# A hybrid decoder block on one core: first steps of the mixer, logits and routing in another order, quad 0's gate tiles cut in 4 KB runs, six tiles queued at the branch

## The chip, the cores and the metric

The kernel runs on one core of a Trainium2 chip. The time is the device time of one execution in microseconds (us). TensorE (PE) multiplies, VectorE (DVE) and ScalarE (ACT) work elementwise, GpSimd (POOL) and SyncE (SP) do side work; both of the last also issue DMA transfers here. Each engine takes its own instructions in the order in which they were laid down, and waits for others through semaphores.

## The reference

For 256 tokens x 1024 the block computes, all in float32 (g_mix, g_sgu, g_ffn, g_ple and g_final are the norms' gains):

```
h = rmsnorm(x, g_mix);  z = h @ w_in
b, c, xin, u, v = split(z, 5 parts of 512)
y_conv = b * conv3(c * xin, w_conv)
y_sgu  = gelu(u) * (causal w_spatial @ layernorm(gelu(v), g_sgu) + b_spatial)
x = x + concat(y_conv, y_sgu) @ w_out
t = rmsnorm(x, g_ffn);  g_prob = softmax(t @ w_group + b_group);  top 1 of 4 groups
e_logits = t @ w_router + b_router;  top 2 of the 8 experts in that group; softmax
x = x + sum over 32 experts of comb * ((silu(t @ w_gate) * (t @ w_up)) @ w_down)
x = x + sigmoid(rmsnorm(x, g_ple) @ w_ple_gate) * (p @ w_ple_proj)
out = rmsnorm(x, g_final)
```

Each expert has a gate and an up matrix of 1024 x 512 and a down matrix of 512 x 1024: 6 MB, and 192 MB for the 32 of them. All are read, whatever the routing.

## The kernel before, in words

**Mixer.** The tokens lie in two tiles (t = 0, 1) of 128 rows. Lines 200 to 211 norm them: ScalarE squares and sums a row block (L204), VectorE and GpSimd make the reciprocal root `rstd` (L114, L115), VectorE scales the identity by it (`diag`, L207), and 16 matmuls with `diag` transpose and scale the tokens at once into `pht` (L210). From `pht` come `hh` and `hl`, a high and a low part (L215, L216); weights are split likewise into `wh` and `wl` by ScalarE and VectorE (or GpSimd; L121, L122), in pieces of 128x1024. Each product is three matmuls: hh x wh, hl x wh, hh x wl. `block_v` makes the 512 columns of v first (48 matmuls into `pv`), then `block_t` the four others (`pz`). Between them stand two small jobs: `stage` (24 rows of gains and taps) is transposed into `pst`, and the spatial weights `wsr` into `pw` (8 transposes), from where VectorE copies them to `wsT` (L299). `junk` and `wsr` share a ring of two buffers (tag `k4`).

**Routing.** After the output projection (`po`, L387 to L389) the residual is added (`x1_add`), transposed (`pxt`), and multiplied with the router weights (`plog`, L477). ScalarE squares the rows for the norm (L472). VectorE then ranks groups and experts, counts each token's place in its expert's list (32 slots an expert), makes a 0/1 matrix `d` (`onehot`, L532), and TensorE gathers the tokens of four experts at a time with it (`pgx`, L543). VectorE also makes the combine weights (L566 to L600). `keep_warm` runs matmuls into a bank that nobody reads.

**Experts.** They go in 8 quads of four. A quad has 12 tiles of 2 MB, 16 KB a partition: 4 of gate (`we0` to `we3`), 4 of up, 4 of down. A tile holds two experts (EP = 2) and half of the contraction, in runs of 8 KB, so that a quad of experts needs a pair of tiles at a time (`granules`). Tiles go through a ring of 6 buffers; in quad 0 three more and one more are there for the up tiles. SyncE issues all of them, each as soon as the tile that held its buffer is used up. The products are `pg` and `pu` (64 matmuls each, L635), `sg` and `hp` on ScalarE and VectorE, `ph` and `hT` (transposes), `pd` (down, 64), `py` (combine).

**Branch.** Were an expert to get more than 32 tokens, further rounds would run; `rounds > 0` is tested once, after quad 1 (L756, L757), by every engine, and is false here. Ahead of it three tiles of quad 2 are issued, two by SyncE and one by GpSimd. The order within an engine is set by the framework's scheduler unless a line is pinned with `keep_in_program_order`; `no_sync_barrier` keeps the work on both sides of it apart.

Of the kernel before, what the change touches and what calls it, by code (L numbers as in the profile page):

```python
# [8 lines left out]
F32 = mybir.dt.float32  # L9
# [3 lines left out]
AF = mybir.ActivationFunctionType  # L13
OP = mybir.AluOpType
# [3 lines left out]
P = 128  # L18
D = 1024
NT = 2  # L20
KC = D // P
# [13 lines left out]
def hymba_conv_sgu_hmoe_block(ctx, tc, a):  # L35
    nc = tc.nc
# [51 lines left out]
    def keep_warm(n):  # L88
        pb = bank("warm")
        for _ in range(n):  # L90
            nc.tensor.matmul(pb[:, 0:P], ident, ident, start=True, stop=True)

    keep_warm(10)

    slot1 = keep.tile([P, CAP], F32, name="slot1")
    nc.gpsimd.iota(slot1, pattern=[[1, CAP]], base=1, channel_multiplier=0,
# [105 lines left out]
    for t in range(NT):  # L202
        junk = fz.tile([P, D], F32, tag="k4", name="junk", bufs=2)
        nc.scalar.activation(junk, xs[:, t], AF.Square, accum_out=stat[:, t:t + 1])  # L204
        rstd_of(stat[:, 2 + t:3 + t], stat[:, t:t + 1], 1.0 / D)
        diag = fz.tile([P, P], F32, tag="diag", name="diag", bufs=2)
        nc.vector.tensor_scalar(diag, ident, stat[:, 2 + t:3 + t], None, op0=OP.mult)  # L207
        for c in range(KC):
            o = (c % 2) * 256 + t * P
            nc.tensor.matmul(pht[c // 2][:, o:o + P], xs[:, t].rearrange("t (p c) -> t c p", c=KC)[:, c], diag,  # L210
                             start=True, stop=True)
    ahead()
    for c in range(KC):
        src = pht[c // 2][:, (c % 2) * 256:(c % 2) * 256 + 256]
# [19 lines left out]
    def block_v():  # L234
        pv = [bank("pv") for _ in range(NT)]
        for c, wh, wl in pieces(512):
            for t in range(NT):
                s = slice(t * P, (t + 1) * P)
                nc.tensor.matmul(pv[t], hh[:, c, s], wh, start=(c == 0), stop=False)
                nc.tensor.matmul(pv[t], hl[:, c, s], wh, start=False, stop=False)  # L240
                nc.tensor.matmul(pv[t], hh[:, c, s], wl, start=False, stop=(c == KC - 1))
        return pv

    def block_t():
# [27 lines left out]
    pv = block_v()  # L272
# [109 lines left out]
    def out_proj(k, wh, wl, ts, first, last):  # L382
        for t in ts:
            s = slice(t * P, (t + 1) * P)
            for h in range(2):
                f = slice(h * 512, (h + 1) * 512)
                nc.tensor.matmul(po[t][h], yh[:, k, s], wh[:, f], start=first, stop=False)  # L387
                nc.tensor.matmul(po[t][h], yl[:, k, s], wh[:, f], start=False, stop=False)
                nc.tensor.matmul(po[t][h], yh[:, k, s], wl[:, f], start=False, stop=last)  # L389
# [15 lines left out]
    def x1_transpose(t):  # L405
        pxt[t] = [bank("pxt") for _ in range(2)]
        for i in range(2):
            for c in range(4):
                nc.tensor.transpose(pxt[t][i][:, c * P:(c + 1) * P],
                                    xs[:, t].rearrange("t (p c) -> t c p", c=KC)[:, 4 * i + c], ident)  # L410

    for n, w in enumerate(rest):
        out_proj(*w, (0,), False, n == 2)
    x1_add(0)
    for n, w in enumerate(rest[:2]):
        out_proj(*w, (1,), False, False)
    x1_transpose(0)
    out_proj(*rest[2], (1,), False, True)
    fy.release()
    xr, xt = pools["xr"], pools["xt"]  # L420

# [5 lines left out]
    fbp = [None]  # L427


    wtiles = {}  # L430

    def load_w(q, i, queue=nc.sync):
        pool = ring if q or i < 4 or i > 7 else xr if i < 7 else x4
        w = slot(f"we{q}_{i}", pool)

        g, n = divmod(i % 4, QE // EP)
        es = slice(q * QE + n * EP, q * QE + (n + 1) * EP)
        if i < 8:
            src = w_gate if i < 4 else w_up
            c = CP * g  # L440
            queue.dma_start(w.rearrange("p (e c f) -> p e c f", e=EP, c=CP), src[:, es, c:c + CP, :])
        else:
            c = CP // 2 * g
            queue.dma_start(w.rearrange("p (e c d) -> p e c d", e=EP, c=CP // 2), w_down[:, es, c:c + CP // 2, :])
        return w

    def granules(q, i0, c_slot):

        for g in range(EP):
            ws = [get_w(q, i0 + g * (QE // EP) + n).rearrange("p (e c f) -> p e c f", e=EP, c=c_slot)  # L450
                  for n in range(QE // EP)]
            for k in range(c_slot):
                yield g * c_slot + k, [ws[j // EP][:, j % EP, k] for j in range(QE)]
# [6 lines left out]

    plog = bank("plog", "L")
    lg = mp.tile([P, NT, 36], F32, name="lg")
    for t in range(NT):
        if t == 1:
            x1_add(t)
            x1_transpose(t)
        h2T = xt.tile([P, KC, P], F32, tag="xT", name="h2T", bufs=2)
        nc.scalar.activation(h2T[:, 0:4].rearrange("p c n -> p (c n)"), pxt[t][0], AF.Copy)
        nc.vector.tensor_copy(h2T[:, 4:8].rearrange("p c n -> p (c n)"), pxt[t][1])
        h3 = h2[:, t].rearrange("t c p -> t p c")  # L470
        x3 = xs[:, t].rearrange("t (p c) -> t p c", c=KC)
        nc.scalar.activation(h3, x3, AF.Square, accum_out=stat[:, 6 + t:7 + t])  # L472
        rs = stat[:, 8 + t:9 + t]
        rstd_of(rs, stat[:, 6 + t:7 + t], 1.0 / D)
        o = plog[:, t * 36:(t + 1) * 36]
        for c in range(KC):
            nc.tensor.matmul(o, h2T[:, c], wr[:, c], start=(c == 0), stop=(c == KC - 1))  # L477
        nc.vector.scalar_tensor_tensor(lg[:, t], o, rs, biasB, op0=OP.mult, op1=OP.add)
    for t in range(NT):

        nc.scalar.activation(h2[:, t].rearrange("t c p -> t p c"), xs[:, t].rearrange("t (p c) -> t p c", c=KC),
                             AF.Copy, scale=stat[:, 8 + t:9 + t])
    keep_warm(24)
    x4 = tc.alloc_tile_pool(name="x4", bufs=1, side="right")


# [75 lines left out]
    xg_next = gather(0, d0)  # L562


    gm = rout[:, :, 0:1]
    nc.vector.tensor_reduce(gm, gl, axis=AX.X, op=OP.max)  # L566
    gd = rout[:, :, 4:8]
# [70 lines left out]
    def gate_up(q, xg, filler=None):  # L638
        pg, pu = bank("pg"), bank("pu")
        for o, i0 in ((pg, 0), (pu, 4)):  # L640
            for c, w in granules(q, i0, CP):
                proj(o, xg, c, w, c == 0, c == KC - 1)
                if filler and c % 2:
                    filler(i0 + c // 2)
        return hidden(pg, pu)
# [11 lines left out]

    def down(q, hT, cm):
        pd = [bank("pd", "L") for _ in range(2)]
        for i, w in granules(q, 8, CP // 2):  # L660
            for h in range(2):
                proj(pd[h], hT, i, [r[:, h * 512:(h + 1) * 512] for r in w], i == 0, i == 3)
        combine(pd, cm)
# [52 lines left out]
    for q in range(NQ):  # L716
# [30 lines left out]
            fb = fbp[0] = tc.alloc_tile_pool(name="fb", bufs=1, side="right")  # L747
        if q == 1:

            for i in range(3):  # L750

                wtiles[q + 1, i] = load_w(q + 1, i, nc.gpsimd if i == 2 else nc.sync)
            qfb = fb.tile([P, NT, NE], F32, name="qfb")
            nc.vector.tensor_copy(qfb, qpos)
            tc.no_sync_barrier()
            rounds = nc.values_load(nover[0:1, 0:1], min_val=0, max_val=7)  # L756
            with tc.If(rounds > 0):  # L757
                with tc.For_i(0, rounds, 1):
                    nc.vector.tensor_scalar(qfb, qfb, -float(CAP), None, op0=OP.add)
                    for fq in range(NQ):  # L760
                        fd = onehot(fq, qfb, fb=True)
                        fxg = gather(fq, fd, fb=True)
                        fcm = spread(fq, fd, fb=True)
                        pg, pu = bank("pg"), bank("pu")
                        fes = slice(fq * QE, (fq + 1) * QE)
                        for o, src in ((pg, w_gate), (pu, w_up)):
                            for c in range(KC):
                                w = fb.tile([P, QE, FE], F32, tag="wfb", name="wfb", bufs=2)
                                nc.sync.dma_start(w, src[:, fes, c, :])
                                proj(o, fxg, c, w, c == 0, c == KC - 1)  # L770
                        fhT = hidden_t(hidden(pg, pu))
                        pd = [bank("pd", "L") for _ in range(2)]
                        for i in range(4):
                            for h in range(2):
                                w = fb.tile([P, QE, FE], F32, tag="wfb", name="wfb", bufs=2)
                                nc.sync.dma_start(w, w_down[:, fes, i, h * 512:(h + 1) * 512])
                                proj(pd[h], fhT, i, w, i == 0, i == 3)
                        combine(pd, fcm)
            tc.no_sync_barrier()
            fb.release()  # L780
# [195 lines left out]
```

## Time and profile before

| | us |
|---|---|
| median of 3 runs | 606.62 (605.61 to 606.96) |
| the profiled execution | 608.43 |
| its span, first to last instruction | 606.7 |
| TensorE busy | 473.5 (78%) |
| VectorE, ScalarE, GpSimd busy | 149.6, 101.6, 45.8 |
| all transfers | 225.07 MB, 371 GB/s over the span |

The timeline names start and length of instructions on one engine, and in brackets how long the engine had been idle and what released it. Times count from the span's start. A stretch's row gives each engine's busy time, the TensorE clock that was granted (1.00 is the upper level), and how busy the 16 DMA engines were (1.0 is all).

### The profile page before, as it was taken

The page shows a single profiled execution, that of the slowest core. Times are in us where ns is not written, and L with a number is a line of the kernel's source. Part 1 is how long each engine was busy: PE and PEld are TensorE (multiplying, and loading weights), DVE is VectorE, ACT ScalarE, POOL GpSimd, SP SyncE. Part 2 cuts the span into 40 slices and gives each one's busy share as a digit, 9 for nine tenths or more (in the row PEclk, how much of TensorE's full clock was granted, in tenths as well). Part 3 has the DMA queues.
Part 4 walks back from the last instruction along what each step waited for, and adds up shares of the span by engine and source line. Part 5 has one row for each costly group of instructions (what it writes and reads, how often), then busy time and mean ns, then how long its engine had stood idle before and what let it go on. Part 6 is the DMA issues. An engine that isn't in the chain of part 4 may idle for free.

```text
span 606.7 us, 6928 instructions
## 1 busy us (share of the span) xinstructions
PE 473.5 (78%) x2955; PEld 243.9 (40%) x2955; DVE 149.6 (25%) x275; ACT 101.6 (17%) x171; POOL 45.8 (8%) x42
## 2 busy tenths in 40 slices
PE   8999999989755776577668965876577666999891
PEld 7799988542311231122213511231123121555471
DVE  2747854422010200120012001200120015410236
ACT  4553545010000000000001200000000005110243
POOL 1533440000000000000000000000000000000003
PEclk8999999999978898988899989877996788899897
DMA  8998669599999799999999999999999999999901
GB/s 310 345 389 336 248 268 421 211 421 407 421 421 420 301 425 420 416 422 420 421 422 423 420 421 421 420 423 420 422 422 422 419 418 407 382 367 369 320 9 69
DMA packets 47048, 225.07 MB, mean 371 GB/s; under 512 B 3204, under 2 KB 15268, under 8 KB 23460
## 3 DMA queue, kind: packets, MB, share of 16 engines
q1 hardware_dynamic: 46740, 222.48, 91.5%
q0 software_dynamic: 272, 2.10, 0.8%
q8 instruction: 24, 0.39, 0.3%
q14 instruction: 12, 0.10, 0.0%
HBM read 223.52 MB, written 1.05 MB: 370 GB/s over the span
## 4 chain that ended last, share of the span: by engine, by line
DMA 39%; PE 20%; DVE 3%; ACT 1%; issue 1%; POOL 1%; SPq 0%; POOLq 0%; ACTq 0%; DVEq 0%
DMA we<-in_w_down_dram 17%; DMA we<-in_w_up_dram 16%; DMA we<-in_w_gate_dram 6%; PE pd L635 5%; PE pu L635 5%; PE pg L635 2%; DVE wlo L680 2%; PE pgg L700 1%; PE pgg L698 1%; PE pgg L699 1%; PE pj L801 1%; PE pgg L890 1%; PE pyw L820 1%; PE pyw L821 1%; PE pyw L822 1%
## 5 line engine op out<-in xcount | busy, mean ns | idle before, releaser
L635 PE MATMUL pu<-we,xg 128*32 128x512 f32 x512 | 84.4, 695 | 35.3 <-DMA we<-in_w_up_dram 33.5
L635 PE MATMUL pd<-we,hT 128*32 128x512 f32 x448 | 81.3, 682 | 34.0 <-DMA we<-in_w_down_dram 22.5
L635 PE MATMUL pg<-we,xg 128*32 128x512 f32 x512 | 77.7, 681 | 27.1 <-DMA we<-in_w_gate_dram 27.1
L635 PEld LDWEIGHTS pd<-we,hT 128*32 128x32 f32 x448 | 19.8, 120 | 90.5 <-issue 39.6
L635 PEld LDWEIGHTS pu<-we,xg 128*32 128x32 f32 x512 | 18.9, 124 | 92.0 <-DMA we<-in_w_up_dram 47.0
L635 PEld LDWEIGHTS pg<-we,xg 128*32 128x32 f32 x512 | 18.4, 121 | 78.8 <-issue 41.1
L115 POOL TENSOR_TENSOR stat<-stat,mhalf 128x1 f32<-128x1 f32 (+1 forms) x9 | 5.9, 660 | 422.7 <-ACT yw L826 403.0
L251 PE MATMUL pz<-hh,wh 128*128 128x256 f32 x128 | 36.2, 283 | 0.7 <-ACT g L264 0.7
L617 DVE TENSOR_TENSOR hp<-sg,pu 128x512 f32<-128x512 f32 x8 | 8.2, 1026 | 113.9 <-PE pu L635 113.9
L253 PE MATMUL pz<-hl,wh 128*128 128x256 f32 x128 | 36.0, 281 | 0.0
L254 PE MATMUL pz<-hh,wl 128*128 128x256 f32 x128 | 36.0, 281 | 0.0
L543 PE MATMUL pgx<-d,h 128*128 128x128 f32 x256 | 30.7, 278 | 2.4 <-DVE d L532 2.4
L543 PEld LDWEIGHTS pgx<-d,h 128*128 128x128 f32 x256 | 29.2, 192 | 7.7 <-issue 3.4
L615 DVE TENSOR_TENSOR sg<-sg,pg 128x512 f32<-128x512 f32 x8 | 5.5, 688 | 108.3 <-ACT sg L614 108.3
L626 ACT ACTIVATE hT<-ph 128x512 f32<-128x512 f32 x8 | 4.8, 597 | 154.9 <-PE ph L624 154.9
L650 DVE COPY ys<-pd 128x512 f32<-128x512 f32 x7 | 4.8, 691 | 94.7 <-PE pd L635 94.7
L655 PE MATMUL py<-ys,cm 128*128 128x512 f32 x56 | 26.3, 609 | 1.5 <-DVE ys L650 1.5
L251 PEld LDWEIGHTS pz<-hh,wh 128*128 128x128 f32 x128 | 24.1, 188 | 1.1 <-ACT g L264 0.9
L254 PEld LDWEIGHTS pz<-hh,wl 128*128 128x128 f32 x128 | 24.1, 188 | 0.0
L253 PEld LDWEIGHTS pz<-hl,wh 128*128 128x128 f32 x128 | 24.1, 188 | 0.0
L614 ACT ACTIVATE sg<-pg 128x512 f32<-128x512 f32 x8 | 4.8, 597 | 110.6 <-PE pg L635 110.6
L649 ACT ACTIVATE ys<-pd 128x512 f32<-128x512 f32 x7 | 4.2, 597 | 104.8 <-PE pd L635 104.8
(233 smaller groups left out, 572.5 us busy)
## 6 DMA issues: line engine op xcount, KB each, us to landing
we<-in_w_up_dram SPq DMA_DIRECT2D x32, 2048.0 KB, 17.8
we<-in_w_gate_dram SPq DMA_DIRECT2D x31, 2048.0 KB, 15.0
we<-in_w_down_dram SPq DMA_DIRECT2D x28, 2048.0 KB, 23.2
wd<-in_w_down_dram SPq DMA_DIRECT2D x12, 512.0 KB, 8.8
wo<-in_w_out_dram SPq DMA_DIRECT2D x2, 2048.0 KB
wpg<-in_w_ple_gate_dram SPq DMA_DIRECT2D x4, 1024.0 KB
w_v<-in_w_in_dram SPq DMA_DIRECT2D x4, 512.0 KB, 8.1
w_c<-in_w_in_dram SPq DMA_DIRECT2D x2, 1024.0 KB
```

Source lines behind the costliest of these rows:

```text
L251: nc.tensor.matmul(o, wh[:, s], hh[:, c], start=(c == 0 and j % 2 == 0), stop=False, skip_group_check=True)
L253: nc.tensor.matmul(o, wh[:, s], hl[:, c], start=False, stop=False, skip_group_check=True)
L254: nc.tensor.matmul(o, wl[:, s], hh[:, c], start=False, stop=last, skip_group_check=True)
L543: nc.tensor.matmul(pg[:, c * P:(c + 1) * P], h2[:, t, 4 * i + c], d[:, t].rearrange("p e s -> p (e s)"), start=(t == 0), stop=(t == NT - 1))
L617: nc.vector.tensor_tensor(hp.rearrange("s c p -> s p c"), sg.rearrange("s (p c) -> s p c", c=4), pu.rearrange("s (p c) -> s p c", c=4), op ...
L635: placed(nc.tensor.matmul(o[rows(j)], xg[:, c, rows(j)], wj, start=first, stop=last, tile_position=(0, j * CAP)))
L655: nc.tensor.matmul(py, cm[:, t], ys[:, f], start=True, stop=True)
L680: nc.vector.scalar_tensor_tensor(wlo[:, 4 * i + c], w[:, f], g, hi[:, f].bitcast(F32), op0=OP.mult, op1=OP.subtract)
L698: nc.tensor.matmul(pgg[t][h], hi[:, s], wh[:, f], start=first, stop=False)
L699: nc.tensor.matmul(pgg[t][h], hi[:, s], wl[:, f], start=False, stop=False)
L700: nc.tensor.matmul(pgg[t][h], lo[:, s], wh[:, f], start=False, stop=last)
L801: nc.tensor.matmul(pj, pT[:, c, t * P:(t + 1) * P], wv[:, c, f], start=(c == 0), stop=(c == 1))
```

## The change

Seven edits: `keep_warm(10)` becomes 14. The tokens are scaled by VectorE (`junk` = xs x rstd, 128x1024) and then transposed with the plain identity. `block_v` takes, within a row c of weights, both token tiles for one kind of product before the next kind. The output projection of t = 1 is finished ahead of the transposes of t = 0; the logits part is written out and pinned, with contiguous writes of the square, and a `keep_warm(24)` becomes 9. A `no_sync_barrier` behind quad 0's gather puts the combine weights after it. Quad 0's gate tiles hold all four experts and a quarter of the contraction, in runs of 4 KB. Ahead of the branch six tiles are issued, two by SyncE and four by GpSimd.

```
-    keep_warm(10)
+    keep_warm(14)
...
-        diag = fz.tile([P, P], F32, tag="diag", name="diag", bufs=2)
-        nc.vector.tensor_scalar(diag, ident, stat[:, 2 + t:3 + t], None, op0=OP.mult)
+        nc.vector.tensor_scalar(junk, xs[:, t], stat[:, 2 + t:3 + t], None, op0=OP.mult)
         for c in range(KC):
             o = (c % 2) * 256 + t * P
-            nc.tensor.matmul(pht[c // 2][:, o:o + P], xs[:, t].rearrange("t (p c) -> t c p", c=KC)[:, c], diag,
-                             start=True, stop=True)
+            nc.tensor.transpose(pht[c // 2][:, o:o + P], junk.rearrange("t (p c) -> t c p", c=KC)[:, c], ident)
...
-            for t in range(NT):
-                s = slice(t * P, (t + 1) * P)
-                nc.tensor.matmul(pv[t], hh[:, c, s], wh, start=(c == 0), stop=False)
-                nc.tensor.matmul(pv[t], hl[:, c, s], wh, start=False, stop=False)
-                nc.tensor.matmul(pv[t], hh[:, c, s], wl, start=False, stop=(c == KC - 1))
+            for n, (h, w) in enumerate(((hh, wh), (hl, wh), (hh, wl))):
+                for t in range(NT):
+                    nc.tensor.matmul(pv[t], h[:, c, t * P:(t + 1) * P], w, start=(c == 0 and n == 0),
+                                     stop=(c == KC - 1 and n == 2))
...
-    for n, w in enumerate(rest[:2]):
-        out_proj(*w, (1,), False, False)
+    for n, w in enumerate(rest):
+        out_proj(*w, (1,), False, n == 2)
     x1_transpose(0)
-    out_proj(*rest[2], (1,), False, True)
...
+    def per_slot(q, i):
+        return 4 if q == 0 and i < 4 else 2
...
+        EP = per_slot(q, i)
+        CP = KC // EP
...
+    x1_rstd(0)
+    h2T_part(0, 0, True)
+    x1_add(1)
+    h2T_part(0, 1, False)
+    x1_rstd(1)
+    x1_transpose(1)
+    h2T_part(1, 0, False)
+    h2T_part(1, 1, True)
+    logits(0, range(KC))
+    logits(1, range(KC))
     for t in range(NT):
...
-    keep_warm(24)
+        norm_rows(t)
+        pin(nc.vector.scalar_tensor_tensor(lg[:, t], plog[:, t * 36:(t + 1) * 36], stat[:, 8 + t:9 + t], biasB,
+                                           op0=OP.mult, op1=OP.add))
+    keep_warm(9)
...
     xg_next = gather(0, d0)
+    tc.no_sync_barrier()
...
-            for i in range(3):
-                wtiles[q + 1, i] = load_w(q + 1, i, nc.gpsimd if i == 2 else nc.sync)
+            for i in range(6):
+                wtiles[q + 1, i] = load_w(q + 1, i, nc.gpsimd if i >= 2 else nc.sync)
```

On TensorE at the start of the program, before (`warm` is keep_warm, `pht` the normed tokens, `pv` and `pz` the products, `pst` and `pw` the small transposes):

```order
L91 MATMUL warm<-ident 128x128 x10
L210 MATMUL pht<-diag,xs 128x128 x16
L239 MATMUL pv<-wh,hh 128x512
L240 MATMUL pv<-wh,hl 128x512
L241 MATMUL pv<-wl,hh 128x512
...
L241 MATMUL pv<-wl,hh 128x512
L291 MATMUL pst<-ident,stage 128x24
L298 MATMUL pw<-ident,wsr 128x128 x8
L251 MATMUL pz<-hh,wh 128x256
```

And now:

```order
L89 MATMUL warm<-ident 128x128 x14
L208 MATMUL pht<-ident,junk 128x128 x16
L236 MATMUL pv<-wh,hh 128x512 x2
L287 MATMUL pst<-ident,stage 128x24
L294 MATMUL pw<-ident,wsr 128x128 x2
L236 MATMUL pv<-wh,hl 128x512 x2
L236 MATMUL pv<-wl,hh 128x512 x2
...
L236 MATMUL pv<-wl,hh 128x512 x2
L294 MATMUL pw<-ident,wsr 128x128 x6
L247 MATMUL pz<-hh,wh 128x256
```

The transpose of `stage` and the first two of `wsr` have moved from behind the 48 matmuls of `block_v` to behind its first two; the other six of `wsr` stay behind them.

On TensorE from the up products of quad 0 to its down products, before (`pgx` is the gather of quad 1, `pc` its combine matrix's transpose):

```order
L635 MATMUL pu<-we_6_1234,xg 32x512 x2
L635 MATMUL pu<-we_7_1236,xg 32x512 x2
L556 MATMUL pc<-ident,d 128x128 x2
L543 MATMUL pgx<-d,h_1014 128x128 x16
L624 MATMUL ph<-ident,hp 128x128 x4
L635 MATMUL pd<-we_8_1298,hT 32x512 x2
```

And now:

```order
L656 MATMUL pg<-we_3_1192,xg 32x512 x8
L656 MATMUL pu<-we_4_1202,xg 32x512 x2
L576 MATMUL pc<-ident,d 128x128 x2
L563 MATMUL pgx<-d,h_1016 128x128 x13
L656 MATMUL pu<-we_5_1204,xg 32x512 x2
...
L656 MATMUL pu<-we_5_1204,xg 32x512 x2
L563 MATMUL pgx<-d,h_1016 128x128 x3
L656 MATMUL pu<-we_6_1222,xg 32x512 x2
...
L656 MATMUL pu<-we_7_1224,xg 32x512 x2
L645 MATMUL ph<-ident,hp 128x128 x4
L656 MATMUL pd<-we_8_1286,hT 32x512 x4
```

The gather of quad 1 has moved from behind the up products to between them, 13 of its matmuls behind the first two.

On SyncE around the branch (`nover` is loaded for its test), before:

```order
L441 DMA we_0_1545<-in_w_gate_dram 128x2x2048
L441 DMA we_1_1547<-in_w_gate_dram 128x2x2048
L756 TENSOR_LOAD nover
L757 COMPARE_AND_BRANCH
...
L441 DMA we_3_3249<-in_w_gate_dram 128x2x2048
L441 DMA we_4_3267<-in_w_up_dram 128x2x2048
L441 DMA we_5_3269<-in_w_up_dram 128x2x2048
L441 DMA we_6_3287<-in_w_up_dram 128x2x2048
```

And now, first on SyncE and then on GpSimd:

```order
L442 DMA we_0_1533<-in_w_gate_dram 128x2x2048
L442 DMA we_1_1535<-in_w_gate_dram 128x2x2048
L777 TENSOR_LOAD nover
...
L778 COMPARE_AND_BRANCH
...
L806 DMA pt_in<-in_p_dram 128x2x256
L442 DMA we_6_3275<-in_w_up_dram 128x2x2048
L442 DMA we_7_3277<-in_w_up_dram 128x2x2048
```

```order
L442 DMA we_2_1537<-in_w_gate_dram 128x2x2048
L442 DMA we_3_1539<-in_w_gate_dram 128x2x2048
L442 DMA we_4_1541<-in_w_up_dram 128x2x2048
L442 DMA we_5_1543<-in_w_up_dram 128x2x2048
L777 TENSOR_LOAD nover
L778 COMPARE_AND_BRANCH
```

Gate tile 3 and up tiles 4 and 5 of quad 2 have moved from SyncE behind the branch to GpSimd ahead of it; SyncE's first expert tile behind the branch is 6.

## Rows read from the trace of the kernel before

**Rows 1.** The page: rate of all transfers in 40 equal slices of the span

```profile
GB/s 310 345 389 336 248 268 421 211 421 407 421 421 420 301 425 420 416 422 420 421 422 423 420 421 421 420 423 420 422 422 422 419 418 407 382 367 369 320 9 69
```

**Rows 2.** Stretches: busy time and instructions by engine, TensorE clock, DMA share, rate

```profile
30.00:98.00 68.00, 68.00 (x503) 63.82 (x502) 42.77 (x62) 29.11 (x33) 26.00 (x13) 1.00 0.82 322
205.00:209.00 4.00, 1.25 (x14) 0.52 (x18) 0.92 (x3) 0.38 (x1) 0.00 (x0) 1.00 0.15 59
209.00:213.00 4.00, 4.00 (x28) 1.09 (x22) 0.00 (x0) 0.00 (x0) 0.00 (x0) 0.57 0.92 326
```

**Rows 3.** Timeline of SyncE, 100 to 160: issues of expert tiles

```profile
118.43 0.88 SPq L444 DMA_DIRECT2D we<-in_w_down_dram  x2
121.86 17.82 SPq L441 DMA_DIRECT2D we<-in_w_gate_dram  x4
```

**Rows 4.** Timeline of TensorE, 5 to 30: start, length, instruction, idle before

```profile
6.62 7.91 PE L210 MATMUL pht<-diag,xs 128*128 128x128 f32 x32 [1.21 <-DVE diag L207]
14.29 0.48 PE L239 MATMUL pv<-wh,hh 128*128 128x512 f32 x1
...
25.34 0.39 PE L241 MATMUL pv<-wl,hh 128*128 128x512 f32 x1
...
25.83 1.10 PE L298 MATMUL pw<-ident,wsr 128*128 128x128 f32 x8
27.60 0.36 PE L251 MATMUL pz<-hh,wh 128*128 128x256 f32 x1 [0.67 <-ACT g L264]
```

**Rows 5.** Timeline of VectorE, 5 to 30

```profile
9.81 1.23 DVE L122 TENSOR_TENSOR wl<-w_v,wh 128x1024 fp32r<-128x1024 f32 x1 [1.66 <-ACT wh L121]
```

**Rows 6.** Instructions on the tile wsr: issue, and time to landing

```profile
L154 SPq DMA_DIRECT2D wsr<-in_w_spatial_dram x1: 395/395/395, 10.0 to 10.0; - x1
...
DMA to landing us min/median/max: 9.9/9.9/9.9
```

**Rows 7.** Timeline of all engines in the routing, 100 to 112

```profile
100.68 1.98 ACT L472 ACTIVATE h<-xs 128x1024 f32<-128x1024 f32 x1
...
103.17 1.97 PE L477 MATMUL plog<-wr,h2T 128*128 128x36 f32 x16 [0.78 <-ACT h2T L468]
...
105.25 0.26 DVE L478 SCALAR_TENSOR_TENSOR lg<-plog,stat,biasB 128x36 f32<-128x36 f32 x1 [2.40 <-PE plog L477]
...
110.46 0.41 DVE L532 TENSOR_TENSOR d<-qpos,slot 128x256 f32<-128x256 f32 x1
```

**Rows 8.** Timeline of TensorE in quad 0, 109 to 146

```profile
114.76 7.07 PE L635 MATMUL pg<-we,xg 128*32 128x512 f32 x64
...
130.18 3.84 PE L543 MATMUL pgx<-d,h 128*128 128x128 f32 x32 [1.11 <-DVE d L532]
...
135.14 7.07 PE L635 MATMUL pd<-we,hT 128*32 128x512 f32 x64 [0.69 <-ACT hT L626]
```

**Rows 9.** The page: costliest groups, two VectorE products of the hidden rows

```profile
L617 DVE TENSOR_TENSOR hp<-sg,pu 128x512 f32<-128x512 f32 x8 | 8.2, 1026 | 113.9 <-PE pu L635 113.9
...
L615 DVE TENSOR_TENSOR sg<-sg,pg 128x512 f32<-128x512 f32 x8 | 5.5, 688 | 108.3 <-ACT sg L614 108.3
```

**Rows 10.** Waits of SyncE, 160 to 215: total, times, longest

```profile
SPq L757 <- SPq L757: 28.5, 4, 8.5
```

**Rows 11.** Timeline of all engines around the branch, 185 to 216

```profile
185.90 0.92 POOL L441 DMA_DIRECT2D we<-in_w_gate_dram  x1 [82.42 <-DMA we<-in_w_down_dram]
...
187.31 1.91 PE L635 MATMUL pd<-we,hT 128*32 128x512 f32 x8 [1.21 <-SPq L757]
...
194.39 5.89 PE L635 MATMUL pd<-we,hT 128*32 128x512 f32 x24 [5.17 <-SPq L757]
...
207.75 0.41 PE L556 MATMUL pc<-ident,d 128*128 128x128 f32 x2 [3.83 <-PEq L757]
208.09 0.40 SPq L441 DMA_DIRECT2D we<-in_w_gate_dram  x1
```

**Rows 12.** Instructions of the branch, line 757: TensorE

```profile
L757 PEldq COMPARE_BRANCH  x1: 5752/5752/5752, 201.7 to 201.7; - x1
```

More of the change, by code (lines that the diff above doesn't have):

```diff
@@ L26 @@
 NQ = NE // QE
-EP = 2
-CP = KC // EP
 EPS = 1e-6
@@ L408, in x1_transpose @@
             for c in range(4):
-                nc.tensor.transpose(pxt[t][i][:, c * P:(c + 1) * P],
-                                    xs[:, t].rearrange("t (p c) -> t c p", c=KC)[:, 4 * i + c], ident)
+                pin(nc.tensor.transpose(pxt[t][i][:, c * P:(c + 1) * P],
+                                        xs[:, t].rearrange("t (p c) -> t c p", c=KC)[:, 4 * i + c], ident))
     for n, w in enumerate(rest):
@@ L445, in load_w, with granules @@
         return w
-    def granules(q, i0, c_slot):
+    def granules(q, i0, c_all):
+        EP = per_slot(q, i0)
+        c_slot = c_all // EP
         for g in range(EP):
@@ L462, in hymba_conv_sgu_hmoe_block @@
     lg = mp.tile([P, NT, 36], F32, name="lg")
-    for t in range(NT):
[L464 to L478, printed above, removed]
@@ L479, in hymba_conv_sgu_hmoe_block, with h2T_part @@
-    for t in range(NT):
-        nc.scalar.activation(h2[:, t].rearrange("t c p -> t p c"), xs[:, t].rearrange("t (p c) -> t p c", c=KC),
-                             AF.Copy, scale=stat[:, 8 + t:9 + t])
-    keep_warm(24)
+    h2T = [xt.tile([P, KC, P], F32, tag="xT", name="h2T", bufs=2) for _ in range(NT)]
+    def h2T_part(t, i, on_act):
+        o = h2T[t][:, 4 * i:4 * i + 4].rearrange("p c n -> p (c n)")
+        pin(nc.scalar.activation(o, pxt[t][i], AF.Copy) if on_act else nc.vector.tensor_copy(o, pxt[t][i]))
@@ new lines, in x1_rstd, with logits, norm_rows @@
+    def x1_rstd(t):
+        pin(nc.scalar.activation(h2[:, t].rearrange("t c p -> t (c p)"), xs[:, t], AF.Square,
+                                 accum_out=stat[:, 6 + t:7 + t]))
+        for i in rstd_of(stat[:, 8 + t:9 + t], stat[:, 6 + t:7 + t], 1.0 / D):
+            pin(i)
+    def logits(t, cs):
+        for c in cs:
+            pin(nc.tensor.matmul(plog[:, t * 36:(t + 1) * 36], h2T[t][:, c], wr[:, c], start=(c == 0),
+                                 stop=(c == KC - 1)))
+    def norm_rows(t):
+        pin(nc.scalar.activation(h2[:, t].rearrange("t c p -> t p c"), xs[:, t].rearrange("t (p c) -> t p c", c=KC),
+                                 AF.Copy, scale=stat[:, 8 + t:9 + t]))
@@ L640, in gate_up @@
         for o, i0 in ((pg, 0), (pu, 4)):
-            for c, w in granules(q, i0, CP):
+            for c, w in granules(q, i0, KC):
                 proj(o, xg, c, w, c == 0, c == KC - 1)
@@ L659, in down @@
         pd = [bank("pd", "L") for _ in range(2)]
-        for i, w in granules(q, 8, CP // 2):
+        for i, w in granules(q, 8, 4):
             for h in range(2):
```

## The prediction

> **What bounds the kernel now.** I read the page's 40 slices first. From the tenth slice on the transfers run near 420 GB/s in nearly every slice up to the tail [rows 1]: there the kernel is bound by the 16 DMA engines, and a tile of 2.1 MB takes 2.1 / 421 = 5.0 us. A stage ahead of that stream is worth what it moves the stream's start; a hole in it is worth its length; a faster TensorE inside it is worth nothing. Two low slices stand out: the eighth (211 GB/s) around the routing, and the fourteenth (301 GB/s) at the branch. Then the stages. From 30 to 98 TensorE is busy 68.00 of 68.00 us at the upper clock level while DMA has a share of 0.82 [rows 2]: the mixer is bound by TensorE, so a delay of its first products is carried to the routing unshrunk. Around the routing the buffers are full, and SyncE issues nothing until 118.43, when TensorE has used up the first gate pair [rows 3]; so the routing's end sets the stream's start. At the branch the stream breaks [rows 2].
>
> **First steps: a gain that turns into a wait.** Now TensorE makes 32 records with `diag` between 6.62 and 14.5, and then 48 matmuls of `block_v` [rows 4]. The change halves the records (plain transposes; eight of `pw` take 1.10, 0.14 each) and puts two VectorE products of 128x1024 in front (1.23 for the nearest, a subtraction of that size [rows 5]). By itself that lets `pv` start some 2 us earlier. But the new order puts `pst` and two of `pw` behind the first two matmuls of `pv`, and `pw` reads `wsr`. That tile is issued at 10.0 and lands 9.9 us later, at 19.9 [rows 6]; nothing ahead of it on SyncE's queue changes. TensorE works in order, so 46 matmuls of `pv` stand behind a transpose that can't start before 19.9, while before, `pw` came at 25.83 and found its data there. What else is queued there doesn't matter to this sum: VectorE's and ScalarE's splits go on, up to their buffers.
> The sum: 19.9 + 2 x 0.14 = 20.2. A matmul of `pv` takes (25.34 - 14.29) / 47 = 0.235, so 46 take 10.8: 31.0. Then six transposes and VectorE's copy, of which four transposes and the copy are on the path: 0.55 + about 0.7, my estimate within the 27.60 - 25.83 = 1.77 that all eight and their copy took: 32.3. `pz` started at 27.60 [rows 4]: 4.7 us later (5.2 with the whole 1.77).
> To this comes the clock. In 205 to 209 TensorE worked 1.25 of 4 us, and then ran four microseconds at a granted 0.57 [rows 2], near its lower level of 1.2 GHz: 4 x 0.43 = 1.7 us lost. Now it idles from about 13 to 19.9. How the clock answers to that is not in the trace of before; bounds are 0 (the clock holds) and 3.4 (that loss twice, for an idle nearly twice as long). I take the row, 1.7. More `keep_warm` at the very start lies ahead of the first transposes and covers none of it. Sum of the first steps: +6.4, between 4.7 and 8.6.
> The Trainium skill bears on this in TensorE: Matmul & The Clock Gate, Step-by-step: what each phase is for: weight loads may be pulled ahead, matmuls keep program order. If it were otherwise the 46 would pass the transpose, which is the first rival's time. No row of before shows a matmul passing a waiting one.
>
> **Logits and routing: earlier.** ScalarE squares t = 1 in 1.98 ahead of the copy `h2T` that the logits wait for, and TensorE idles 0.78 in front of `plog` [rows 7]. In the new order the copies of t = 1 don't stand behind that long strided write, so I count 0.8. From the logits at 105.25 to `d` at 110.46 VectorE takes 5.2 us [rows 7], with 14 instructions of the combine weights strewn in, which now come behind the gather. Most of them fill waits between dependent steps; I take 0.5, between 0 and 1.4. The cut of `keep_warm` to 9 shortens nothing that is waited for. Sum: -1.3, between -0.3 and -2.2.
>
> **Quad 0.** A gate tile with all four experts is used up after 16 matmul records instead of a pair after 32, so the first refill goes out 1.7 us sooner (a quarter of 7.07 instead of half [rows 8]). That is worth nothing: behind the four tiles whose buffers become free, the next issue waits for the first half of the down products. It is one of the last two of the four SyncE issues of gate tiles, which stretch over 17.82 us from 121.86 and so end at 139.7, right after half of the `pd` that began at 135.14 [rows 3, 8]. The stream is set by `pd`. Runs of 4 KB instead of 8 concern four tiles that are loaded in the mixer, where DMA has room [rows 2]: 0; were that cover gone, a tile is 5.0 us, a few tenths of it at most.
> The gather of quad 1, however, now stands between the up products. Its `d` waits on VectorE behind the product `sg` (0.69 [rows 9]), and that behind ScalarE's pass over the finished `pg` (taken as long). So two matmuls after the gate TensorE waits 0.6 + 0.7 + 0.4 less 0.3 = 1.4 us. Before, the gather was hidden better: 1.11 idle in front of it [rows 8], and its 3.84 us covered `hp` (1.03 [rows 9]). Now nothing covers `hp`, and TensorE waits 1.2 for it. Against the 1.11 that goes: +1.5. Bounds are 0 (another order of arrivals) and 2.6 (both waits in full).
>
> **The branch: a hole that closes.** SyncE's way past the branch waits until its own transfers have landed: 28.5 us in four waits [rows 10], and its next issue is at 208.09 [rows 11], when its queue is empty. In 205 to 209 the transfers ran at 59 GB/s, in 209 to 213 at 326 [rows 2]: against 421 that is 4 x (1 - 59/421) + 4 x (1 - 326/421) = 4.3 us of stream lost. GpSimd's issue took 0.92 at 185.90 [rows 11]. Now it queues four tiles, three more than before, 15 us of transfers, and two of them as soon as the down products of quad 1 end. These move while SyncE waits. SyncE's two tiles share the engines with them and land later. While GpSimd's one tile moved, successive down tiles released TensorE at 187.31 and 194.39, 7.1 apart instead of 5.0 [rows 11]; with that ratio the second gate tile lands about 209.5 instead of 207.3, and quad 2 starts some 2 us later. The queue holds work to about 222, SyncE's tile 6 is issued near 216: no hole. I take -4.3, between -3.4 (the 59 GB/s part alone) and -4.7.
> The Trainium skill, in DMA: Bandwidth & Descriptors, Queues, rings and completion order, says that an engine alternates between the queues that hold work. By equal turns the two tiles would have been 10 us apart; the trace shows 7.1, and decides. By equal turns SyncE's tiles would land near 214, which still leaves no hole, but little room.
>
> **Sum.** +6.4 - 1.3 + 1.5 - 4.3 = +2.3. Against the profiled execution's own 608.43 (span 606.7) that is 610.7; that execution lies 1.8 above the median of the runs, 606.62, so I forecast 608.9 for the median.
>
> **Rivals.**
> First, no stall: `wsr` is there, or TensorE passes the transpose. Then the first steps give 2 us: -2 - 1.3 + 1.5 - 4.3 = -6.1, 600.5, faster. For it speaks that the drawn edit is shorter; against it stand the issue at 10.0 and the 9.9 us [rows 6], with DMA loaded all the while. It decides if `wsr` lands before 13. 0.11.
> Second, the stall is there but the clock holds, and routing and gather come out at their good ends: +4.7 - 1.8 + 1.0 - 4.3 = -0.4, 606.2, no change. The clock of 1.00 within 205 to 209 speaks for it, the 0.57 behind it against. 0.16.
> Third, the hole stays: TensorE's branch took 5.75 us at 201.7 [rows 12], in a stretch where one queue moved. If that grows beside full queues, so that quad 2 starts after some 217, tile 6 comes too late and the 4.3 are lost again: +6.6, 613.2, slower. Its own 3.83 us of idle [rows 11] shows that the branch is slow; nothing shows that it grows by 9. 0.10.
> The forecast keeps 0.63, with its own range of 606.8 to 611.0.
>
> **How the numbers follow.** A measurement can tell about 0.2%, 1.2 us, from no change. Slower by more: the forecast above 607.8 (0.50 of its 0.63) and the third rival, 0.60. Same: 0.12 of the second, 0.11 of the forecast, 0.23. Faster: the first rival, 0.04 of the second, 0.02 of the forecast, 0.17. For 8 in 10 the range leaves out the first rival and most of the third: 603.8 to 612.4.
>
> **What would show it.** In the profile after, TensorE idle from about 13 to 19.9, released by `wsr`, `pz` at 32 to 35 and a granted clock below 1 behind 20; then the mixer as before, 5 to 7 late. The first gate product near 114.76 + 5. An idle of over 1 us two matmuls into `pu`, and again in front of `ph`. Near the branch no stretch of 4 us under 400 GB/s, and SyncE's first issue behind it later than 208.09 by more than the shift. I am wrong if `pz` starts ahead of 30, or if the slice at the branch stays low.

## The result, and the profile after

| | before | after |
|---|---|---|
| median, us | 606.67 (605.61 to 607.64, 5 runs) | 610.99 (610.48 to 612.55, 5 runs) |
| ratio | | 1.0074, 95% interval 1.0056 to 1.0093 |
| profiled execution, its span | 608.43, 606.7 | 611.05, 609.3 |
| granted clock, mean | 0.914 | 0.904 |

The change makes the kernel 4.3 us slower, which is clear of no change; 608.9 was forecast, in a range of 603.8 to 612.4. The profiled execution of after (611.05) is one of the median, that of before lies 1.8 above its own. So the two spans differ by only 2.6 us; the two traces are compared stage by stage, and the sum is held against the medians.

The page's row of transfers in 40 slices, of after, answers to [rows 1]:

```profile
GB/s 312 347 389 326 139 210 368 386 331 297 421 422 419 423 416 415 421 419 423 420 422 422 420 423 421 421 422 421 420 422 422 421 419 415 413 353 380 329 38 69
```

The hole in the fourteenth slice (301 before) is gone, and a weak ninth and tenth slice (331, 297) stand where the stream began before: it begins later.

The timeline of after, first steps, one instruction of ScalarE and then TensorE (start, length, instruction, in brackets the idle before and its releaser), answers to [rows 4, 6]:

```profile
8.52 1.06 ACT L202 ACTIVATE junk<-xs 128x1024 f32<-128x1024 f32 x1 [3.17 <-PE pht L208]
...
11.33 1.97 PE L208 MATMUL pht<-ident,junk 128*128 128x128 f32 x8 [2.85 <-DVE junk L205]
12.96 1.20 PE L236 MATMUL pv<-wh,hh 128*128 128x512 f32 x2
18.45 0.27 PE L287 MATMUL pst<-ident,stage 24*128 24x24 f32 x1 [4.29 <-DMA stage<-in_g_ple_dram]
19.57 0.66 PE L294 MATMUL pw<-ident,wsr 128*128 128x128 f32 x2 [0.86 <-DMA wsr<-in_w_spatial_dram]
...
32.65 0.82 PE L294 MATMUL pw<-ident,wsr 128*128 128x128 f32 x6
33.91 0.36 PE L247 MATMUL pz<-hh,wh 128*128 128x256 f32 x1 [0.44 <-DVE wsT L295]
```

The second token tile's `junk` waits until the transposes of the first have read theirs, and TensorE idles 2.85 in front of the second half of `pht`. Then come two matmuls of `pv`, and TensorE waits for `stage` until 18.45 and for `wsr` until 19.57; `pz` starts at 33.91 instead of 27.60.

Stretches of after (busy time by engine, the granted clock third from the end, DMA share, GB/s); the first three answer to the last row of [rows 2], the other two are the routing:

```profile
14.00:20.00 6.00, 0.85 (x5) 0.63 (x4) 3.55 (x7) 3.17 (x6) 2.35 (x1) 0.50 1.09 357
20.00:24.00 4.00, 4.00 (x12) 3.13 (x11) 0.00 (x0) 0.27 (x1) 0.00 (x0) 0.50 1.05 379
24.00:28.00 4.00, 4.00 (x19) 3.22 (x18) 1.23 (x1) 1.86 (x2) 0.08 (x1) 0.98 1.10 285
111.00:115.00 4.00, 0.70 (x7) 0.50 (x5) 3.55 (x19) 0.12 (x1) 0.00 (x0) 0.74 1.01 428
115.00:119.00 4.00, 3.06 (x18) 2.99 (x18) 0.77 (x4) 0.00 (x0) 0.00 (x0) 0.50 1.01 424
```

The granted clock is 0.50, the lower of its two levels, through the idle and for 4 us behind it. It is there again at 115 to 119, after a stretch in which TensorE was busy for 0.70 of 4 us.

The timeline of TensorE in after from the logits to the down products of quad 0 answers to [rows 7, 8]:

```profile
110.56 1.14 PE L89 MATMUL warm<-ident 128*128 128x128 f32 x8
115.07 0.21 PE L541 MATMUL ppos<-sel,before 128*128 128x32 bf16 x1 [3.37 <-DVE sel L536]
...
116.30 5.46 PE L563 MATMUL pgx<-d,h 128*128 128x128 f32 x32 [0.87 <-DVE d L552]
121.69 7.07 PE L656 MATMUL pg<-we,xg 128*32 128x512 f32 x64
128.58 1.03 PE L656 MATMUL pu<-we,xg 128*32 128x512 f32 x4
...
130.54 3.17 PE L563 MATMUL pgx<-d,h 128*128 128x128 f32 x26 [0.56 <-DVE d L552]
133.64 3.63 PE L656 MATMUL pu<-we,xg 128*32 128x512 f32 x28
...
143.01 0.63 PE L645 MATMUL ph<-ident,hp 128*128 128x128 f32 x4 [1.31 <-DVE hp L638]
144.32 7.10 PE L656 MATMUL pd<-we,hT 128*32 128x512 f32 x64 [0.69 <-ACT hT L647]
```

With nine warming matmuls TensorE runs out at 111.7 and idles 3.37 ahead of the counting; the gather of quad 0 then takes 5.46 instead of 3.81. Before `ph` there is a wait of 1.31 for `hp` that was not there, and from the first gate product to the first down product it is 22.63 us instead of 20.38.

The timeline of all engines around the branch in after, and SyncE's waits there (total, times, longest), answer to [rows 10, 11]:

```profile
195.30 1.65 POOL L442 DMA_DIRECT2D we<-in_w_gate_dram  x2 [87.66 <-DMA we<-in_w_down_dram]
...
203.35 6.17 PE L656 MATMUL pd<-we,hT 128*32 128x512 f32 x24 [4.71 <-SPq L778]
...
209.04 1.52 POOL L442 DMA_DIRECT2D we<-in_w_up_dram  x2 [12.09 <-PE pd L656]
...
217.98 1.92 PE L656 MATMUL pg<-we,xg 128*32 128x512 f32 x4
...
223.18 9.50 PE L656 MATMUL pg<-we,xg 128*32 128x512 f32 x58 [3.28 <-SPq L778]
223.83 0.40 SPq L806 DMA_DIRECT2D pt_in<-in_p_dram  x1
```

```profile
SPq L778 <- SPq L778: 34.6, 4, 9.9
```

GpSimd issues two tiles at 195.30 and two more at 209.04. TensorE is past the branch and begins `pg` at 217.98 with four matmul records, and then waits till 223.18 for SyncE's second gate tile. SyncE's waits grow from 28.5 to 34.6, the longest to 9.9.

### The profile page after: what moved, and what is told of

It reads as the page before. It is cut to its first block, busy times and chain, and to the rows that moved or that the text cites. A ratio compares the mean times of both kernels' runs of the same rounds, so it can differ in the third digit from the quotient of the medians.

```text
span 609.3 us, 6856 instructions
## 1 busy us (share of the span) xinstructions
PE 471.9 (77%) x2917; PEld 241.6 (40%) x2917; DVE 154.0 (25%) x275; ACT 100.0 (16%) x171; POOL 49.1 (8%) x45
## 3 DMA queue, kind: packets, MB, share of 16 engines
HBM read 223.52 MB, written 1.05 MB: 369 GB/s over the span
## 4 chain that ended last, share of the span: by engine, by line
DMA 35%; PE 25%; ACT 1%; issue 1%; POOL 1%; DVE 0%; POOLq 0%; ACTq 0%
DMA we<-in_w_down_dram 19%; DMA we<-in_w_up_dram 11%; PE pg L656 6%; PE pd L656 5%; DMA we<-in_w_gate_dram 5%; PE pu L656 5%; PE pgg L719 1%; PE pgg L720 1%; PE pgg L721 1%; PE pj L822 1%; PE pgg L911 1%; PE pyw L841 1%; PE pgx L563 1%; PE py L676 1%; PE pyw L842 1%
## 5 line engine op out<-in xcount | busy, mean ns | idle before, releaser
L656 PE MATMUL pd<-we,hT 128*32 128x512 f32 x448 | 83.2, 686 | 35.7 <-DMA we<-in_w_down_dram 24.5
L656 PE MATMUL pu<-we,xg 128*32 128x512 f32 x512 | 82.2, 673 | 27.1 <-DMA we<-in_w_up_dram 25.4
L656 PE MATMUL pg<-we,xg 128*32 128x512 f32 x512 | 80.5, 697 | 29.2 <-DMA we<-in_w_gate_dram 25.9
L563 PEld LDWEIGHTS pgx<-d,h 128*128 128x128 f32 x256 | 31.0, 201 | 8.7 <-issue 6.3
L563 PE MATMUL pgx<-d,h 128*128 128x128 f32 x256 | 32.9, 288 | 1.4 <-DVE d L552 1.4
```

The source lines that it names most:

```text
L563: nc.tensor.matmul(pg[:, c * P:(c + 1) * P], h2[:, t, 4 * i + c], d[:, t].rearrange("p e s -> p (e s)"), start=(t == 0), stop=(t == NT - 1))
L656: placed(nc.tensor.matmul(o[rows(j)], xg[:, c, rows(j)], wj, start=first, stop=last, tile_position=(0, j * CAP)))
```

## The experiments

**At the branch alone.** The kernel before with this one edit:

```
-            for i in range(3):
-                wtiles[q + 1, i] = load_w(q + 1, i, nc.gpsimd if i == 2 else nc.sync)
+            for i in range(6):
+                wtiles[q + 1, i] = load_w(q + 1, i, nc.gpsimd if i >= 2 else nc.sync)
```

> The kernel before with the one change at the branch: six tiles of quad 2 queued, two by SyncE, four by GpSimd. Theory (the hole of 4.3 us at the branch closes, and nothing else moves): no stretch of 4 us under 400 GB/s between 200 and 225, the stream's end 4.3 to 5.0 us earlier, 601.7 to 602.4. Rival (SyncE's tiles land later beside GpSimd's and the hole only moves, or the pieces that now follow cost it again): less than half, above 604.5.

Measured: 601.80 against 607.00 (ratio 0.9924, 0.9909 to 0.9939). Its stretches where before had 59 and 326 GB/s, and TensorE's first gate products of quad 2:

```profile
201.00:205.00 4.00, 2.69 (x7) 0.90 (x6) 2.76 (x4) 0.00 (x0) 0.08 (x1) 1.00 1.01 420
205.00:209.00 4.00, 0.81 (x4) 0.35 (x6) 0.86 (x3) 0.31 (x1) 0.00 (x0) 0.96 1.01 412
209.00:213.00 4.00, 1.35 (x4) 0.00 (x0) 0.06 (x1) 0.08 (x1) 0.00 (x0) 0.50 1.02 418
```

```profile
208.53 1.82 PE L635 MATMUL pg<-we,xg 128*32 128x512 f32 x4
214.31 8.90 PE L635 MATMUL pg<-we,xg 128*32 128x512 f32 x58 [3.97 <-SPq L757]
```

No hole, though SyncE's second tile releases TensorE as late as 214.31. The edit is worth 5.2 us by the two medians and 4.6 by the ratio, with an interval of 3.7 to 5.5. The other way round, the changed kernel with three tiles:

```
-            for i in range(6):
-                wtiles[q + 1, i] = load_w(q + 1, i, nc.gpsimd if i >= 2 else nc.sync)
+            for i in range(3):
+                wtiles[q + 1, i] = load_w(q + 1, i, nc.gpsimd if i == 2 else nc.sync)
```

> The changed kernel with three tiles queued at the branch, as before the change. Theory (the hole at the branch is worth the same in both surroundings, 5.2 us by the experiment on the kernel before): a stretch of about 4 us with almost no transfers behind 215, time 611.0 + 4.3 to 5.2 = 615.3 to 616.2, from its ratio to the kernel before 1.4 to 1.6% slower. Rival (in the changed kernel the later stream start already covers part of the hole): below 613.5.

Measured: 615.60, ratio 1.0157 (1.0137 to 1.0176). The hole is back in its stretches:

```profile
213.00:217.00 4.00, 0.70 (x2) 0.00 (x0) 1.75 (x4) 0.00 (x0) 0.00 (x0) 0.86 0.54 219
217.00:221.00 4.00, 3.39 (x18) 1.09 (x22) 0.43 (x1) 0.38 (x1) 0.00 (x0) 0.50 0.58 180
```

Against the 1.0074 of after it is 0.83%, 5.0 us: within the noise the same worth in both surroundings. Against 421 GB/s these two stretches lose 4.2 us of stream, and before's lost 4.3.

The spans of the traces say so too. From the first down product of quad 0 to the end it takes 464.7 us (the kernel before with six tiles) and 465.0 (after); with three tiles it takes 469.2 (the changed kernel) and 468.9 (the kernel before with the 4 KB runs, below). That is 3.9 to 4.5 us. In the trace of before it takes 471.6, so that is where its 1.8 us above the median lie.

**The stall behind wsr.** The changed kernel with the order of `pv`, `pst` and `pw` pinned (`pin(...)` around their matmuls and transposes, three lines):

> The changed kernel with the matmuls of block_v and the transposes of stage and wsr pinned in program order, so that pst and all eight pw stand behind pv again; nothing else moves on any engine but one copy on VectorE. Theory (the stall behind wsr is a delay that the mixer, bound by TensorE, carries to the end unshrunk): pv runs on from about 13, pz starts between 26.0 (upper clock throughout) and 27.7 (1.7 us lost to the lower level after the idle in front of the second pht) instead of 33.9, the first gate product comes as much earlier, and the time falls by 6.2 to 7.9 us, to 603.1 to 604.8. Rival (the mixer has slack, or the weights' arrival takes the place of wsr): pz is earlier, but the gate product by less than half of that, and the time stays above 607.

Measured: 605.06, ratio 0.9969 (0.9954 to 0.9983). TensorE's `pw` and `pz`, then gather, gate and down of quad 0:

```profile
26.46 1.09 PE L294 MATMUL pw<-ident,wsr 128*128 128x128 f32 x8
27.99 0.36 PE L247 MATMUL pz<-hh,wh 128*128 128x256 f32 x1 [0.44 <-DVE wsT L295]
```

```profile
110.38 6.59 PE L563 MATMUL pgx<-d,h 128*128 128x128 f32 x32 [0.87 <-DVE d L552]
116.91 7.07 PE L656 MATMUL pg<-we,xg 128*32 128x512 f32 x64
...
139.54 8.79 PE L656 MATMUL pd<-we,hT 128*32 128x512 f32 x64 [0.69 <-ACT hT L647]
```

`pz` comes 5.92 earlier than in after, 0.3 later than the late end of what was expected, and the time falls by 1.05% of before, 6.4 us: the delay is carried through the mixer, not absorbed. `pz` is still 0.4 later than before: without the stall, the first steps as the change has them gain nothing, since the 2.85 us in front of the second half of `pht` are there in this trace too. In this execution (607.92, the highest of twelve) only 4.8 us are left at the gate, since the gather takes 6.59 at the lower clock, and `pd` 8.79. The twelve runs lie in two groups of six, 603.2 to 604.2 and 605.9 to 607.9, and the median falls between them, so the 6.4 us are known to a microsecond or two only. I take the clock in these two places for the difference, which is not shown, as only the upper group has a trace.

Next a third buffer, on top of the pins:

```
-    wsr = fz.tile([P, 8, P], F32, tag="k4", name="wsr", bufs=2)
+    wsr = fz.tile([P, 8, P], F32, tag="k4", name="wsr", bufs=3)
...
-        junk = fz.tile([P, D], F32, tag="k4", name="junk", bufs=2)
+        junk = fz.tile([P, D], F32, tag="k4", name="junk", bufs=3)
```

> The changed kernel with pst and pw pinned behind pv, as in the first experiment, and a third buffer for junk and wsr, so that the second token tile needn't wait for the transposes of the first. Theory (the first steps as drawn do give about 2 us once neither pw nor the ring holds TensorE): no idle of 2.85 in front of the second half of pht, pv from about 11, pz near 25.5 (27.99 with the pins alone, 27.60 before), time 2 to 2.5 us under that of the pins alone, about 603. Rival (the arrival of w_v or the splits of hh and hl hold pv back instead): pz stays at 27.5 or later, 605.

Measured: 602.66, ratio 0.9917 (0.9898 to 0.9936). TensorE's second half of `pht`, first `pv`, `pw` and `pz`:

```profile
8.61 1.15 PE L208 MATMUL pht<-ident,junk 128*128 128x128 f32 x8 [0.40 <-DVE junk L205]
10.04 0.73 PE L236 MATMUL pv<-wh,hh 128*128 128x512 f32 x2 [0.28 <-ACT hh L212]
...
22.44 1.09 PE L294 MATMUL pw<-ident,wsr 128*128 128x128 f32 x8
23.97 0.36 PE L247 MATMUL pz<-hh,wh 128*128 128x256 f32 x1 [0.44 <-DVE wsT L295]
```

With the third buffer the first steps are worth more than I had thought: `pz` at 23.97 is 3.6 us ahead of before, and the time falls by 3.2 us against the pins alone, where 2 to 2.5 were expected. Moreover, with the third buffer and no pins, a version that was not timed, the scheduler lays down the same order on every engine. So the ring of two, in which `junk` now stays in use up to the transposes, is what makes the scheduler hoist `pst` and `pw`; by what rule, I haven't followed. What `keep_warm(14)` and the new order within `block_v` add to the 3.6 us was not run by itself.

**The warming matmuls.** The changed kernel with `keep_warm(24)` for `keep_warm(9)`:

> The changed kernel with keep_warm(24) instead of keep_warm(9) behind the logits. Theory (with 9, TensorE runs dry 3.4 us ahead of the counting matmuls and the gather of quad 0 then runs at the lower clock level, 5.46 us instead of 3.81): the gather takes 3.8 again, the first gate product comes 1.6 us earlier (120.1) and the time falls by 1.6 to about 609.4. Rival (VectorE's chain sets the start, the clock costs nothing that is waited for): no change, 611.0; or the longer warming stands in front of the counting matmuls and costs up to 1 us.

Measured: 610.20, ratio 1.0058 (1.0042 to 1.0073). TensorE's gather, gate and down products, and a stretch at the start of `pd`:

```profile
116.07 3.81 PE L563 MATMUL pgx<-d,h 128*128 128x128 f32 x32 [0.87 <-DVE d L552]
119.81 7.07 PE L656 MATMUL pg<-we,xg 128*32 128x512 f32 x64
...
142.44 8.79 PE L656 MATMUL pd<-we,hT 128*32 128x512 f32 x64 [0.69 <-ACT hT L647]
```

```profile
142.00:146.00 4.00, 3.56 (x20) 1.12 (x24) 0.09 (x1) 0.39 (x1) 0.00 (x0) 0.57 0.35 145
```

The gather takes 3.81 again and the gate comes 1.9 earlier (1.6 expected). The same holds over all traces: the five with `keep_warm(9)` idle 3.4 us and then take 5.2 to 6.6 for this gather, the seven with 24 take 3.81. But the time falls by about 1.0 only, within the two intervals: `pd` now takes 8.79 with the clock at 0.57 in its first 4 us, and SyncE's four gate issues, which wait for its first half, end at 148.7 instead of 148.9. In this trace the clock's loss moved from one place to the next.

**The gather between the up products.** The changed kernel with a scheduling barrier:

```
         if q == 0:
+            tc.no_sync_barrier()
             cm = spread(q, d)
```

> The changed kernel with a scheduling barrier between quad 0's up products and the gather of quad 1, so that the gather stands behind the up products again. Theory (the gather between the up products costs an uncovered wait for d and one for hp, 2.2 us by the two traces): the distance from the first gate product to the first down product falls from 22.6 to between 20.4 and 21.4 us (VectorE now makes d behind hp, which before it did not wait for in full), time 608.8 to 609.8. Rival (the distance is set by the arrival of the tiles, not by the order): no change, 611.0.

Measured: 608.56, ratio 1.0047 (1.0023 to 1.0072). TensorE's first gate and down products:

```profile
121.56 7.07 PE L656 MATMUL pg<-we,xg 128*32 128x512 f32 x64
...
142.78 7.10 PE L656 MATMUL pd<-we,hT 128*32 128x512 f32 x64 [0.69 <-ACT hT L647]
```

21.2 us between them, within the expectation, and by the medians 2.7 thousandths of before or 1.6 us. The intervals overlap: four of the seven runs lie at 607.7 to 608.6, three at 610.9 to 612.3 beside those of after. So the shorter distance is shown by the trace, its worth in time only roughly. Both repairs together, with the barrier behind `spread` and `keep_warm(24)`, and the stall left in:

> The changed kernel with keep_warm(24) and the gather of quad 1 held behind the up products by a barrier behind quad 0's combine matrix; the stall behind wsr stays. In the trace with keep_warm(24) alone the first gate product came 1.9 us earlier, but the down products ran 1.7 us longer, 0.57 of the clock in their first 4 us, and the stream began no earlier. Theory (the uncovered wait in front of ph lets the clock fall there, and with the gather in that place it does not): pd takes 7.1, the first gate product comes 1.9 us earlier and pd 2.0 to 2.2 sooner behind it, time 611.0 - 1.9 - 2.1 = 607.0. Rival (the clock falls in pd for another reason, or something else sets the stream): pd takes 8.8 again, 608.6 or more.

Measured: 609.05, ratio 1.0030 (1.0020 to 1.0040). TensorE's gate and down products:

```profile
120.88 7.07 PE L656 MATMUL pg<-we,xg 128*32 128x512 f32 x64
...
142.50 7.10 PE L656 MATMUL pd<-we,hT 128*32 128x512 f32 x64 [0.69 <-ACT hT L647]
```

`pd` takes 7.10. Over all traces, with the gather between the up products `pd` takes 8.79 in three (the pins, the pins with a third buffer, `keep_warm(24)`) and 7.10 in two (after, and after with three tiles); with the gather behind them it takes 7.07 to 7.10 in all seven. So the lower clock came only with the gather's place, but not each time. The sum was missed by 2 us: behind this barrier the distance is 21.6, not 20.5, and `pz` began at 34.76 in this execution, 0.85 later than in after, mostly because the lower clock lasted longer behind the stall (0.52 still in 22 to 26).

**Quad 0's gate tiles.** The kernel before with `per_slot` and the 4 KB runs alone:

> The kernel before with the one change to quad 0's gate tiles (four experts and a quarter of the contraction a tile, runs of 4 KB). Theory (the stream behind quad 0 is set by the first half of the down products, so an earlier refill is worth nothing): the first refill is issued 1.7 us earlier, the third gate tile of quad 1 at the same time as before (138.8), no change, 606.9 within 0.2%. Rival (the earlier refill moves the stream): 1.7 us less, 605.2; second rival (shorter runs slow the loads): above 608.

Measured: 606.35, ratio 0.9993 (0.9979 to 1.0007): no change. SyncE's issues, answering to [rows 3]:

```profile
116.92 2.08 SPq L448 DMA_DIRECT2D we<-in_w_down_dram  x2
120.35 20.03 SPq L445 DMA_DIRECT2D we<-in_w_gate_dram  x4
```

The refill goes out 1.5 us earlier, and the four gate issues end at 140.4 instead of 139.7: nothing is gained.

**All repairs.** The changed kernel with pins, third buffer, `keep_warm(24)` and the barrier behind `spread`:

> The changed kernel with all four repairs: pins, third buffer, keep_warm(24), and a scheduling barrier behind quad 0's combine matrix that holds the gather of quad 1 behind the up products. Theory (the terms add up: against the kernel before -2.1 from the first steps, -1.0 from the routing, 0 to +0.5 from quad 0, -5.2 from the branch): first gate product near 111.7, first down product 20.4 to 20.9 later, no lower clock in pd, 598.5 to 599.3. Rival (what is gained ahead of the stream is taken back by the DMA, which has to bring quad 0's tiles by then, or at the branch): 601.5 or more, no better than the kernel before with the branch change alone (601.8).

Measured: 598.00, ratio 0.9853 (0.9836 to 0.9870). TensorE's first gate and down products:

```profile
109.82 7.08 PE L656 MATMUL pg<-we,xg 128*32 128x512 f32 x64
...
131.44 7.10 PE L656 MATMUL pd<-we,hT 128*32 128x512 f32 x64 [0.69 <-ACT hT L647]
```

The sum holds with two terms off in opposite directions: the gate comes 1.9 earlier than expected (the third buffer gave more than 2.1), and the down product 21.6 behind it, not 20.4 to 20.9. Next the same with no barrier at all: the one that the change put behind quad 0's gather is what moved quad 1's gather; without it the scheduler leaves that behind the up products.

```
     xg_next = gather(0, d0)
-    tc.no_sync_barrier()
```

> The combined version with the scheduling barrier behind quad 0's gather taken out instead of a second barrier put in; quad 1's gather then stands behind the up products by the scheduler's own choice, and the combine weights are made within the routing again. Theory (the barrier behind the gather gains at most 0.5 us in the routing, and its absence brings the distance from gate to down back from 21.6 to 20.4 us): first gate product 0.2 to 0.6 later than in the combined version (110.0 to 110.4), down 0.6 to 1.0 earlier, time 597.0 to 597.6. Rival (the combine weights hold up VectorE's chain by more than 1 us, or the product pc waits longer behind the up products): 598.0 or more.

Measured: 596.88, ratio 0.9847 (0.9834 to 0.9860). TensorE's gate, gather and down products in this last version:

```profile
109.70 7.07 PE L655 MATMUL pg<-we,xg 128*32 128x512 f32 x64
...
125.12 3.84 PE L563 MATMUL pgx<-d,h 128*128 128x128 f32 x32 [1.11 <-DVE d L552]
...
130.08 7.07 PE L655 MATMUL pd<-we,hT 128*32 128x512 f32 x64 [0.69 <-ACT hT L646]
```

20.38 between gate and down as before, and the gate at 109.70, where 110.0 to 110.4 were expected. From `pz` to the gather of quad 0 it takes 82.55 us here and 82.39 with both barriers: putting the combine weights behind that gather bought 0.16 us, not 0.5, while the two barriers cost 1.24 in quad 0 (21.62 against 20.38). Both versions beat the kernel before by 9 us and the changed kernel by 13 to 14; the intervals don't part them from each other.

## Why the prediction was right

| term | predicted | traces and runs |
|---|---|---|
| first steps, at `pz` | +6.4 | +6.3 |
| logits and routing, at the start of `pgx` | -1.3 | -1.0 |
| the gather of quad 0 itself | 0 | +1.65 |
| gate to down in quad 0 | +1.5 | +2.25 |
| the branch | -4.3 | -3.9 to -5.2 |
| sum | +2.3 | +4.0 to +5.3; medians +4.3 |

The direction came by the mechanism that was forecast, the stall, but the size did not: 610.99 stands at the very end of the forecast's own range (606.8 to 611.0), because one term had been put at nothing and another was too small.

- First steps: right in mechanism and size. The wait was read from the order and the landing of `wsr` [rows 6], which came 9.8 us after its issue (9.9 before), and no matmul passed the waiting transposes. The clock was 0.50 for 4 us, 2.0 us lost where 1.7 were taken. The pins show that the stall is the cause, as 6.4 us come back with it. Two waits were not foreseen, for `stage` and for the ring ahead of the second half of `pht`; both end ahead of the one for `wsr`, which hides them here.
- Routing: the gain is there (TensorE reaches the gather 5.28 later, not 6.31), but its split was not as forecast: the combine weights account for 0.16 of it, not 0.5. The mis-sized step is the sentence that the cut of `keep_warm` to 9 "shortens nothing that is waited for". True of the wait, but those matmuls also held the clock for the gather: 1.65 us. I had priced the clock for one idle stretch and not looked for others that the change opens.
- Quad 0: the 4 KB tiles were worth nothing, as forecast for the reason given. The gather's price was 2.25 instead of 1.5, inside the bounds of 0 to 2.6, and not for the reasons given alone. The wait for `hp` is as forecast (1.31 against 1.2), that for `d` shows as 0.56 idle. The prediction left out that the cut pieces take longer, start to next start: the first four records of `pu` take 0.96 where the whole group of 64 needs 0.44 for four, the next 28 take 3.55 instead of 3.08, and the gather in two pieces 3.97 instead of 3.67; together 1.3 us. Why is not shown.
- The branch: closed as forecast. My ratio of 7.1 to 5.0 for tiles that share the engines was wrong for the two gate tiles, the equal turns were right: the second came at 214.31, not 209.5, when only the branch was changed. As the prediction noted, that still leaves no hole. The runs put its worth at 4.6 to 5.2 and the spans of the traces at 3.9 to 4.5: the 4.3 that was forecast lies among them, and nothing shows clear of noise that the bound of 4.7 was passed.
- The first rival priced the first steps without the stall at a gain of 2 us, and so did the sentence that "by itself" the change lets `pv` start that much earlier. Both are wrong for the kernel as it stands: with the stall taken out `pz` is 0.4 later than before, and only a third buffer makes it 3.6 earlier. The third rival did not come: TensorE's branch took 6.13 us beside full queues instead of 5.75.

## What to carry to other kernels

Look at where the scheduler puts an instruction that waits for a load, above all after a tile in a small ring gets a longer life: here transposes laid down early held 46 matmuls for 5.9 us (19.89 in after, 14.01 with the pins), and a third buffer gives the order back. Matmuls that seem only to pass time are paid for by what follows at the upper clock; before taking some away, see what runs behind the gap. And time each part of a bundle by itself: here one edit of -4 to -5 us was covered by three effects of +9 to +10 together.

## What the runs showed of the hardware

- The Trainium skill, in DMA: Bandwidth & Descriptors, Queues, rings and completion order, has each DMA engine alternate between the queues that hold work. In after the last two tiles of SyncE beside GpSimd's queue took 9.9 us each (203.35 to 223.18), where one alone takes 5.0 at 421 GB/s, so the trace agrees there. The tile ahead of them, behind GpSimd's first issue, took 6.6 (196.72 to 203.35), and before, beside a single tile of GpSimd, it was 7.1; why these are shorter is not shown.
- A wait of 1.31 and one of 0.69 around four transposes were followed by 8.79 us of `pd` in three traces (a clock of 0.57 over the first 4 us with `keep_warm(24)`) and by 7.10 us at the upper level in two, the changed kernel itself among them. What decides between the two stays open.
